# Gate rows spread over the partitions by a stride-zero DRAM read, with each head's exponent and mask taken into the head before

## The chip, the cores and the metric

One core of a Trainium2 chip runs the kernel. The metric is the device time of one execution in microseconds (us). The engines are named as in the profile: PE (TensorE, matmuls; PEld its weight loads), ACT (ScalarE), DVE (VectorE), POOL (GpSimd), SP (SyncE, which here only issues DMA transfers). Transfers are also issued by ACT.

## The reference

One encoder layer over 2048 prompt tokens and 64 sample tokens, model width 1024. Four pooling channel groups and four mLSTM heads of width 128 share one input projection and one output projection; a gated feed-forward part with a causal convolution follows. The change concerns the mLSTM:

```
b    = cumsum(log_sigmoid(f gate));  dmat[t,s] = b[t] - b[s] + ig[s]   (s <= t)
inter = b + m;  m_t = max(inter, max_s dmat)
wt   = exp(dmat - m_t)
a    = wt * (q . k)
num  = a @ v + exp(inter - m_t) * (C q);   den likewise with n
h    = num / max(|den|, exp(-m_t))
C, n are carried from chunk to chunk
```

Then each head is normalized and multiplied by the sigmoid of the o projection. The kernel splits dmat - m_t into a part per row (b - m_t at t, called r) and a part per column (ig - b at s): wt[s,t] = exp(r[t] + c[s]), with chunks of 128 tokens.

## The kernel before, in words

The attention phase takes the first 735 us of the span. It handles the tokens in four groups of 512 (the last with the 64 sample tokens besides, 576 columns). The feed-forward phase fills the rest and isn't touched.

All large products are made as three fp32r matmuls of high and low halves (`gemm`, line 460). A weight block arrives as `raw` by a DMA on SP, ACT copies it to its high half (line 394) and DVE subtracts to get the low half (line 397); `work_out` does this some blocks ahead.

For each group, `proj_v` makes v for all heads (`va`) and the gate columns. Then the generator `gate_rows` turns the gates into rows of 4 heads x 512 tokens, in small steps: r, the running maximum M, and the columns `CL` (c, and three exponentials) and `GL` (the chunk's carry factor on all partitions). For each head, `proj_qko` makes q, k and th (tanh of o), evacuated from PSUM by ACT (line 1246), and the generator `lstm` does the head's own work. Both generators stand in a queue bg[0]; `gemm` calls `tick(0)` at five places of a weight row, and each tick runs one step, up to the next `yield`. So a head's lstm lies between the matmuls of the next head's projections, and gate_rows between those of the first head's. Other queues hold the pooling, the next group's norm, and, on DVE, the sums of conditioning weights (`ada`, line 210). `fold` (lines 887, 888: 8 small products with WPT, folded into w_out) runs beside group 0 only, in steps taken by `extra()`.

In lstm, r has to stand on all 128 partitions. It does so by a matmul (line 1292): the one-hot column `E_r[:, hd]`, taken with stride zero as a 128-column weight, times `RHL`, where rows 0 to 3 hold the high half of r and rows 32 to 35 its low half. ACT takes Exp of the product from PSUM for each of four chunks, with the column c as its bias, into `at`; DVE takes the minimum with a causal mask. Then come, in order: transposes of k (line 1305) and `kw` on DVE, q.k (line 1315) and at times it; the products kw with va that advance the state (line 1330, `st`); the products of state and at with q and va (lines 1350, 1352), from which ACT and DVE make `nd`; a square `jk` on ACT for each chunk; the scale `sf` (DVE, and a power on POOL); nd times sf. The closing transposes of nd (line 1384) are done by `end()`, which is kept in `ends` and called in the next head.

PSUM: four large banks for projections (mm_ps), and four single ones for everything else (m2_ps, `m` in the profile), which are handed out in turn: the k-th request waits until the (k-4)-th has been read. Instructions wrapped in `Urgent` are shown at line 233. Group 0 is placed by a scheduler on its estimates; the work of groups 1 to 3 follows mostly the order of the code.

Of the kernel before, what the change touches and what calls it, by code (L numbers as in the profile page):

```python
# [9 lines left out]
F32 = mybir.dt.float32  # L10
F32R = mybir.dt.float32r
AF = mybir.ActivationFunctionType
# [53 lines left out]
def tile_layer(ctx: ExitStack, tc: tile.TileContext, xT, vecs, cst, rst, w_mod, w_ada, c_rows, w_qkou, w_v, w_pool,  # L66
# [21 lines left out]
    def m2_ps():  # L88
        return bank("m2")
# [11 lines left out]
    def scr():  # L101
        return sp.tile([P, TMAX], F32, tag="scr", name="scr")
# [717 lines left out]
    if True:  # L820
# [270 lines left out]
        E_r = a1.tile([P, NH], F32R, tag="E_r", name="E_r")  # L1091
        R4 = a1.tile([P, TMAX], F32, tag="R4", name="R4")
        pool.memset(R4, 0.0)
        RHL = a1.tile([P, TMAX], F32R, tag="RHL", name="RHL")
        pool.memset(RHL.bitcast(F32), 0.0)
# [65 lines left out]
        def gate_rows(o, gt, cols):  # L1161
# [53 lines left out]
            act.activation(RHL[0:4, :T], r[:4, :T], AF.Copy)  # L1215
            dve.tensor_tensor(out=RHL[32:36, :T], in0=r[:4, :T], in1=RHL[0:4, :T].bitcast(F32), op=ALU.subtract)
            for _ in range(8):
                yield
# [21 lines left out]
            cols += [CL, GL]  # L1240
# [32 lines left out]

        ends = []

        def lstm(o, hd, qko, va, cols, mix):
# [3 lines left out]
            CL, GL = cols  # L1280
            at = a2.tile([P, WIDE], F32, tag="at", name="at")
            if o.last:
                pool.memset(at[TS:, GT:TMAX], 0.0)
                pool.memset(at[:, TMAX:], 0.0)
# [4 lines left out]
            for (a, b, n, s) in o.tsegs:  # L1289
                lo, w = a * P, (b - a) * n  # L1290
                pr = m2_ps()
                pe.matmul(pr[:n, :w], E_r[:, hd:hd + 1].broadcast_to([P, n]), RHL[:, lo:lo + w], start=True, stop=True)
                for ti in range(a, b):
                    c0 = (ti - a) * n
                    act.activation(at[:n, ti * P:ti * P + n], pr[:n, c0:c0 + n], AF.Exp, bias=CL[:n, ti, 0, hd:hd + 1])

                av = at[:n, lo:lo + w].rearrange("p (t c) -> p t c", c=n)
                dve.tensor_tensor(out=av, in0=av, in1=mask[:n, :n].unsqueeze(1).broadcast_to([n, b - a, n]), op=ALU.min)
            if o.last:
                yield  # L1300
# [20 lines left out]
            extra()  # L1321
            yield
# [42 lines left out]
            for (a, b, n, s) in o.tsegs:  # L1365

                den = nd[:n, a:b, 128]
                dve.tensor_tensor(out=sf[:n, a:b], in0=den, in1=den, op=ALU.mult)
                dve.tensor_tensor(out=sf[:n, a:b], in0=sf[:n, a:b], in1=CL[:n, a:b, 2, hd], op=ALU.max)
                dve.scalar_tensor_tensor(out=sf[:n, a:b], in0=sf[:n, a:b], scalar=EPS, in1=sq[:n, a:b],  # L1370
                                         op0=ALU.mult, op1=ALU.add)
                pool.tensor_tensor(out=sf[:n, a:b], in0=sf[:n, a:b], in1=half[:n, :b - a], op=ALU.pow)
# [81 lines left out]
        for o in groups:  # L1454
# [16 lines left out]
            if o.g == 0:  # L1471
                t = scr()
                nc.sync.dma_start(out=t[:P, :NH], in_=cst[:P, NCST + 512:NCST + 512 + NH])
                dve.tensor_copy(E_r, t[:P, :NH])
# [757 lines left out]
def _constants():  # L2232
    c = np.zeros((P, NCST + 512 + NH), np.float32)
# [8 lines left out]
    for h in range(NH):  # L2242
        c[h, NCST + 512 + h] = c[32 + h, NCST + 512 + h] = 1.0
# [72 lines left out]
```

## Time and profile before

| what | value |
|---|---|
| time, median of 3 runs | 2164.13 us (2162.03 to 2164.81) |
| the profiled execution: its time, its span | 2170.81 us, 2169.0 us |
| granted TensorE clock, mean | 0.998 |
| PE busy | 2143.5 us, 99% of the span |
| DVE, ACT, POOL busy | 1629.1 us (75%), 1096.2 us (51%), 250.5 us (12%) |
| the broadcast matmuls (line 1292) | 20, 0.40 us long each for 512 columns |
| the Exps of `at` | 68 instructions, 19.0 us |
| DMA in the attention phase | 215.83 MB, 294 GB/s |

The profiled execution is the one that the rows come from; its own time stands 6.7 us over the median of the runs. A row of the timeline begins with its start in us from the span's start and its duration; in brackets stand the idle time of the engine before it and what ended it. In a list of waits the numbers are us in total, how many times, and the longest. A row of line 233 is told apart by its tiles: `at<-m,CL` is the Exp, `at<-at,mask` the mask, `kw<-m,CL` the weighting of k.

### The profile page before, as it was taken

Reading aid. Unit: us, or ns where it says so; the run is one execution under the profiler, and the core shown is the slowest. Engines: PE = TensorE matmul, PEld = TensorE weight load, DVE = VectorE, ACT = ScalarE, POOL = GpSimd, SP = SyncE. Lnnn points to the kernel's source line nnn. Section 1 sums busy time; section 2 is a strip of 40 time slices with the busy share of each in tenths; the row PEclk is TensorE's granted clock in tenths of the full one; section 3 lists DMA queues with packets and bytes.
Section 4 is the critical chain, followed back from the end, with each engine's and each line's share of the span. In section 5 each row is a group of like instructions: output and inputs, shape, how many; then the busy total and the mean of one; then the engine's idle time right before and its main releaser. Section 6 shows DMA issues by size and latency. Waiting matters only on the chain.

```text
span 2169.0 us, 37946 instructions
## 1 busy us (share of the span) xinstructions
PE 2143.5 (99%) x13488; PEld 2042.9 (94%) x13488; DVE 1629.1 (75%) x3068; ACT 1096.2 (51%) x2182; POOL 250.5 (12%) x499
## 2 busy tenths in 40 slices
PE   8999999999999999999999999999999999999998
PEld 7788988888899999999999999999999999999998
DVE  5678768767964868797957668988876597887874
ACT  4555235334333546464736455655655365565554
POOL 0000000002000101010101120100100331111112
PEclk9999999999999999999999999999999999999999
DMA  8897998988886576889977976666678675555542
GB/s 306 305 327 256 336 338 279 354 319 292 279 306 221 168 261 219 303 279 313 331 225 244 322 265 196 229 224 199 221 232 264 217 260 183 174 174 189 174 160 79
DMA packets 245862, 543.63 MB, mean 251 GB/s; under 512 B 25252, under 2 KB 68772, under 8 KB 242856
## 3 DMA queue, kind: packets, MB, share of 16 engines
q1 hardware_dynamic: 236232, 518.89, 70.6%
q10 hardware_dynamic: 9440, 22.32, 2.6%
q8 instruction: 106, 1.74, 0.3%
q14 instruction: 84, 0.69, 0.1%
HBM read 415.12 MB, written 125.99 MB: 249 GB/s over the span
## 4 chain that ended last, share of the span: by engine, by line
PE 71%; DVE 8%; DMA 4%; issue 2%; ACT 2%; SPq 0%; POOL 0%; DVEq 0%; POOLq 0%; ACTq 0%
PE mm L1595 33%; PE mm L460 14%; PE mm L2161 12%; PE mm L2038 8%; DVE wt L397 2%; DMA wt<-wsum 1%; PE mm L1129 1%; DMA raw<-w_ada 1%; DVE tg L1573 1%; ACT tg L1568 0%; PE m L1350 0%; PE m L1330 0%; PE m L1352 0%; DVE scr L233 0%; DMA wsum<-w 0%
## 5 line engine op out<-in xcount | busy, mean ns | idle before, releaser
L1595 PE MATMUL mm<-hx,wt 128*128 128x352 f32 x5544 | 888.6, 321 | 1.6 <-DVE eg L1604 1.6
L1595 PEld LDWEIGHTS mm<-hx,wt 128*128 128x128 f32 x5544 | 881.9, 188 | 2.9 <-ACT wt L394 1.3
L460 PE MATMUL mm<-hl,wt 128*128 128x512 f32 (+2 forms) x1920 | 388.4, 357 | 0.8 <-ACT va L233 0.8
L394 ACT ACTIVATE wt<-raw 128x512 fp32r<-128x512 f32 (+3 forms) x470 | 276.8, 597 | 169.6 <-PE mm L2161 47.7
L460 PEld LDWEIGHTS mm<-hl,wt 128*128 128x128 f32 x1920 | 315.7, 189 | 43.9 <-ACT va L233 1.0
L397 DVE TENSOR_TENSOR wt<-raw,wt 128x512 fp32r<-128x512 f32 (+3 forms) x470 | 312.7, 671 | 47.8 <-ACT wt L394 47.0
L2161 PE MATMUL mm<-av,wt 128*128 128x448 f32 (+1 forms) x1632 | 262.7, 322 | 0.0
L2161 PEld LDWEIGHTS mm<-av,wt 128*128 128x128 f32 x1632 | 250.4, 188 | 11.1
L2010 DVE SCALAR_TENSOR_TENSOR x<-mm,MOD,x 128x352 f32<-128x352 f32 (+3 forms) x360 | 167.4, 504 | 78.6 <-PE mm L2161 65.1
L2038 PE MATMUL mm<-av,wt 128*128 128x352 f32 x1344 | 220.8, 323 | 2.5 <-DVE ea L1604 0.9
L2038 PEld LDWEIGHTS mm<-av,wt 128*128 128x128 f32 x1344 | 215.4, 188 | 5.6 <-DVE ea L1604 3.6
L1642 ACT ACTIVATE mm<-mm 128x352 f32<-128x352 f32 x196 | 87.8, 448 | 250.3 <-PE mm L1595 194.0
L460 PE MATMUL mm<-mx,wt 128*128 128x512 f32 (+1 forms) x960 | 183.1, 352 | 0.4 <-DVE scr L233 0.3
L460 PEld LDWEIGHTS mm<-mx,wt 128*128 128x128 f32 x960 | 159.4, 189 | 23.3 <-issue 0.5
L1573 DVE SCALAR_TENSOR_TENSOR ta<-ea,V,ta 128x704 f32<-128x704 f32 (+1 forms) x132 | 125.7, 952 | 64.4 <-ACT ta L1568 51.6
L1573 DVE SCALAR_TENSOR_TENSOR tg<-eg,V,tg 128x704 f32<-128x704 f32 (+1 forms) x132 | 125.7, 952 | 62.0 <-ACT tg L1568 59.7
L397 DVE TENSOR_TENSOR wt<-wt 128x512 fp32r<-128x512 f32 x196 | 132.8, 684 | 12.9 <-ACT wt L394 12.9
L394 ACT ACTIVATE wt<-wt 128x512 fp32r<-128x512 f32 x196 | 119.8, 623 | 36.2 <-DMA wt<-wsum 32.0
L1551 POOL COPY ea<-UC 128x2 f32<-128x2 f32 x66 | 32.9, 499 | 484.8 <-DVE ta L1573 397.0
L1782 ACT ACTIVATE tg<-tg 128x704 f32<-128x704 f32 (+1 forms) x66 | 52.5, 795 | 71.2 <-DVE tg L1573 71.2
L1129 PE MATMUL mm<-wt,hl 128*128 128x256 f32 (+1 forms) x576 | 71.1, 284 | 0.0
L1129 PEld LDWEIGHTS mm<-wt,hl 128*128 128x128 f32 x576 | 70.3, 190 | 0.6 <-issue 0.4
(298 smaller groups left out, 2173.5 us busy)
## 6 DMA issues: line engine op xcount, KB each, us to landing
wt<-wsplit SPq DMA_DIRECT2D x132, 512.0 KB, 4.5
raw<-w_up SPq DMA_DIRECT2D x198, 256.0 KB, 4.0
wt<-hl_kept SPq DMA_DIRECT2D x96, 512.0 KB, 5.9
wt<-wsum SPq DMA_DIRECT2D x132, 256.0 KB, 4.9
wsplit<-wt SPq DMA_DIRECT2D x66, 512.0 KB, 5.5
w<-w_up SPq DMA_DIRECT2D x44, 512.0 KB, 5.1
wsum<-w SPq DMA_DIRECT2D x22, 1024.0 KB, 4.8
Bd<-fscr ACTq DMA_DIRECT2D x56, 352.0 KB, 4.3
```

Source lines behind the costliest of these rows:

```text
L394: act.activation(u.w[:, 0, :u.n], u.raw[:, :u.n], AF.Copy)
L397: dve.tensor_tensor(out=u.w[:, 1, :u.n], in0=u.raw[:, :u.n], in1=u.w[:, 0, :u.n].bitcast(F32), op=ALU.subtract)
L460: pe.matmul(ps[bi][:, :hi - lo], U[:, a, k % 4 * P:(k % 4 + 1) * P], mv[k][:, b, lo:hi], start=(at == 0 and pi == 0), stop=(k == order[-1] ...
L1129: pe.matmul(ps[ti][:n, :cols], h[4 * kh + k4][:, b, lo:lo + n], U[:, a, k4 % 2 * cols:(k4 % 2 + 1) * cols], start=(kh == 0 and k4 == 0 and ...
L1551: pool.tensor_copy(ext[:, 0:2], UC[:, f, :])
L1573: dve.scalar_tensor_tensor(out=t[:, :E], in0=ext[:, j:j + E], scalar=wc(j, f), in1=t[:, :E], op0=ALU.mult, op1=ALU.add)
L1595: pe.matmul(bk.t[:, :FH], U[:, a, kc * P:(kc + 1) * P], Bo.at(nm, kc, b), start=(first and kc == 0 and pi == 0), stop=(kc == 3 and pi == 2 ...
L1642: act.activation(to.t[:, :FH], bk.t[:, :FH], AF.Copy)
L1782: act.activation(self.tg[:, :E], self.tg[:, :E], AF.Silu)
L2010: dve.scalar_tensor_tensor(out=x3[n][:, a:b], in0=bk.t[:, a - lo:b - lo], scalar=gt2(n, s), in1=x3[n][:, a:b], op0=ALU.mult, op1=ALU.add)
L2038: pe.matmul(bk.t[:, :FH], U[:, a, c:c + P], quad.put(op, m, b), start=(first and m == 0 and pi == 0), stop=(m == 1 and pi == 2), skip_grou ...
L2161: pe.matmul(bks[i].t[:, :hi - lo], U[:, a, k % 4 * P:(k % 4 + 1) * P], av[k][:, b, lo:hi], start=(k == 0 and (a, b) == PASSES[0]), stop=(k ...
```

## The change

`gate_rows` writes r to a DRAM buffer `rd` by a DMA that ACT issues, where it wrote RHL. `at_tile` loads one head's row of rd into an SBUF tile on all 128 partitions: the source is taken with stride zero, 256 KB arrive (and 64 x 64 more in the last group). `decay` takes the Exp in place, SBUF to SBUF, and the mask. For head 0 the load is issued four steps after the write and decay stands at the end of gate_rows; for head hd+1 the load is issued in head hd's lstm after `extra()`, and decay stands at the end of head hd's lstm. RHL, E_r, their preparation, the 20 matmuls and one `yield` of the last group are gone, and with them one request of a small bank for each head (two in the last group).

```diff
-            act.activation(RHL[0:4, :T], r[:4, :T], AF.Copy)
-            dve.tensor_tensor(out=RHL[32:36, :T], in0=r[:4, :T], in1=RHL[0:4, :T].bitcast(F32), op=ALU.subtract)
-            for _ in range(8):
+            rd = dr.tile([4, TMAX], F32, tag=f"rd{o.g}", name=f"rd{o.g}")
+            act.dma_start(out=rd[:, :T], in_=r[:4, :T])
+            for _ in range(4):
+                yield
+            spread = [at_tile(o, rd, 0)]
+            for _ in range(4):
                 yield
...
-            cols += [CL, GL]
+            cols += [CL, GL, rd, spread]
+            decay(o, spread[0], CL, 0)
...
+        def at_tile(o, rd, hd):
+
+            load = Urgent(nc.scalar).dma_start
+            t = a2.tile([P, WIDE], F32, tag="at", name="at")
+            if o.last:
+                load(out=t[:, :GT], in_=rd[hd:hd + 1, :GT].broadcast_to([P, GT]))
+                load(out=t[:TS, GT:TMAX], in_=rd[hd:hd + 1, GT:TMAX].broadcast_to([TS, TS]))
+                pool.memset(t[TS:, GT:TMAX], 0.0)
+                pool.memset(t[:, TMAX:], 0.0)
+            else:
+                load(out=t[:, :o.T], in_=rd[hd:hd + 1, :o.T].broadcast_to([P, o.T]))
+            return t
+
+        def decay(o, at, CL, hd):
+
+            for (a, b, n, s) in o.tsegs:
+                lo, w = a * P, (b - a) * n
+                for ti in range(a, b):
+                    cell = at[:n, ti * P:ti * P + n]
+                    tc.keep_in_program_order(nc.scalar.activation(cell, cell, AF.Exp, bias=CL[:n, ti, 0, hd:hd + 1]))
+                av = at[:n, lo:lo + w].rearrange("p (t c) -> p t c", c=n)
+                tc.keep_in_program_order(nc.vector.tensor_tensor(
+                    out=av, in0=av, in1=mask[:n, :n].unsqueeze(1).broadcast_to([n, b - a, n]), op=ALU.min))
...
-            for (a, b, n, s) in o.tsegs:
-                lo, w = a * P, (b - a) * n
-                pr = m2_ps()
-                pe.matmul(pr[:n, :w], E_r[:, hd:hd + 1].broadcast_to([P, n]), RHL[:, lo:lo + w], start=True, stop=True)
-                for ti in range(a, b):
-                    c0 = (ti - a) * n
-                    act.activation(at[:n, ti * P:ti * P + n], pr[:n, c0:c0 + n], AF.Exp, bias=CL[:n, ti, 0, hd:hd + 1])
-
-                av = at[:n, lo:lo + w].rearrange("p (t c) -> p t c", c=n)
-                dve.tensor_tensor(out=av, in0=av, in1=mask[:n, :n].unsqueeze(1).broadcast_to([n, b - a, n]), op=ALU.min)
-            if o.last:
-                yield
...
             extra()
+            if hd < NH - 1:
+                spread.append(at_tile(o, rd, hd + 1))
             yield
...
+            if spread:
+                decay(o, spread[0], CL, hd + 1)
```

In the order of the instructions, the first place is ACT in group 0, from the row r being ready to the first head's Exp (`rd` is the DRAM buffer, `scr_725` and `scr_731` hold r, `raw` and `wt` are weight blocks). Before:

```order
L233 ACTIVATE RHL_183<-scr_731 4x512
L394 ACTIVATE wt_863<-raw_796 128x512
L394 ACTIVATE wt_901<-raw_821 128x512
L1246 ACT_TABLE_LOAD
L1246 ACTIVATE th_843<-mm_844 128x512
L233 ACTIVATE CL_883<-m2_885 128x4x4 x3
L394 ACTIVATE wt_919<-raw_848 128x512
L394 ACTIVATE wt_967<-raw_866 128x512
L1246 ACTIVATE q_899<-mm_900 128x512
L233 ACTIVATE at_979<-m2_982,CL_883 128x128 x4
```

And now:

```order
L233 DMA rd0_807<-scr_725 4x512
L394 ACTIVATE wt_859<-raw_790 128x512
L233 DMA at_851<-rd0_807 128x512
L394 ACTIVATE wt_897<-raw_815 128x512
L233 DMA at_995<-rd0_807 128x512
L1247 ACT_TABLE_LOAD
L1247 ACTIVATE th_837<-mm_838 128x512
L233 ACTIVATE CL_879<-m2_881 128x4x4 x3
L394 ACTIVATE wt_915<-raw_842 128x512
L1294 ACTIVATE at_851<-at_851,CL_879 128x128 x4
L394 ACTIVATE wt_968<-raw_862 128x512
L1247 ACTIVATE q_895<-mm_896 128x512
```

The write of r stands where the copy into RHL stood, the loads for heads 0 and 1 stand between the weight copies behind it, and the Exps of head 0 stand ahead of one weight copy and the q evacuation that they followed before.

The second place is PE in group 0, from the fold's first two blocks to head 0's closing transposes (`q_713` and `q_707` are head 0's q, `q_899` and `q_895` head 1's; `nd_981` is head 0's result). Before:

```order
L887 MATMUL m2_1018<-w4_767,WPT_177 128x128 x4
L1350 MATMUL m2_1053<-st2_1013,q_713 128x129
L1352 MATMUL m2_1053<-va_689,at_979 128x129
L460 MATMUL mm_1145<-hl6_577,wt_1117 128x512 x2
L887 MATMUL m2_1072<-w4_767,WPT_177 128x128 x4
L1315 MATMUL m2_1174<-q_899,k_965 128x128 x4
L1330 MATMUL m2_1194<-va_689,kw_1159 128x129
L1384 MATMUL mm_1181<-V_96,nd_981 128x128 x4
```

And now:

```order
L887 MATMUL m2_1013<-w4_761,WPT_177 128x128 x4
L1362 MATMUL m2_1040<-SP0_184,q_707 128x129
L1364 MATMUL m2_1040<-va_686,at_851 128x129
L1362 MATMUL m2_1040<-st0_1004,q_707 128x129
L460 MATMUL mm_1145<-hl7_575,wt_1117 128x512
L887 MATMUL m2_1067<-w4_761,WPT_177 128x128 x4
L460 MATMUL mm_1145<-hl7_575,wt_1117 128x512 x2
L1315 MATMUL m2_1160<-V_96,k_966 128x128 x4
L1342 MATMUL m2_1188<-va_686,kw_1158 128x129 x3
L1342 MATMUL m2_1198<-va_686,kw_1158 128x129
L1399 MATMUL mm_1173<-V_96,nd_981 128x128 x4
```

Behind the first fold block stood head 0's last two products, and now stand its first three, with head 1's transposes of k, its four kw products and head 0's closing transposes behind the second block.

The third place is ACT at the same point in the program (`sq` gathers a chunk's sum of squares; line 888 evacuates the fold, line 908 squares the next group's x). Before:

```order
L888 ACTIVATE w4_767<-m2_1018 128x512
L233 ACTIVATE nd_981<-m2_1053 128x129
L233 ACTIVATE jk_1070,sq_1044<-nd_981 128x128
L888 ACTIVATE w4_767<-m2_1072 128x512
L394 ACTIVATE wt_1216<-raw_1096 128x512
```

And now:

```order
L888 ACTIVATE w4_761<-m2_1013 128x512
L233 DMA at_1183<-rd0_807 128x512
L233 ACTIVATE nd_981<-m2_1040 128x129
L888 ACTIVATE w4_761<-m2_1067 128x512
L233 ACTIVATE jk_1053,sq_1039<-nd_981 128x128
L394 ACTIVATE wt_1210<-raw_1091 128x512
L233 ACTIVATE jk_1057,sq_1039<-nd_981 128x128
L908 ACTIVATE ssum_1077<-mx0_948 128x512
L233 ACTIVATE jk_1061,sq_1039<-nd_981 128x128
L908 ACTIVATE mx0_948<-mx0_948 128x512
L233 ACTIVATE jk_1065,sq_1039<-nd_981 128x128
```

One of head 0's four squares stood here, and now all four stand here, between other instructions and behind the load for head 2.

More of the change, by code (lines that the diff above doesn't have):

```diff
@@ L1090, in tile_layer @@
         mask = a1.tile([P, P], F32, tag="mask", name="mask")
-        E_r = a1.tile([P, NH], F32R, tag="E_r", name="E_r")
         R4 = a1.tile([P, TMAX], F32, tag="R4", name="R4")
         pool.memset(R4, 0.0)
-        RHL = a1.tile([P, TMAX], F32R, tag="RHL", name="RHL")
-        pool.memset(RHL.bitcast(F32), 0.0)
         M = a1.tile([4, TMAX + 2], F32, tag="M", name="M")
@@ L1279, in lstm @@
             q, k, th = qko
-            CL, GL = cols
-            at = a2.tile([P, WIDE], F32, tag="at", name="at")
-            if o.last:
-                pool.memset(at[TS:, GT:TMAX], 0.0)
-                pool.memset(at[:, TMAX:], 0.0)
+            CL, GL, rd, spread = cols
+            at = spread.pop()
             kw = a2.tile([P, 5, P], F32, tag="kw", name="kw", bufs=1)
@@ L1288, in lstm @@
             nd = a2.tile([P, 5, 129], F32, tag="nd", name="nd")
-            for (a, b, n, s) in o.tsegs:
-                lo, w = a * P, (b - a) * n
-                pr = m2_ps()
-                pe.matmul(pr[:n, :w], E_r[:, hd:hd + 1].broadcast_to([P, n]), RHL[:, lo:lo + w], start=True, stop=True)
-                for ti in range(a, b):
-                    c0 = (ti - a) * n
-                    act.activation(at[:n, ti * P:ti * P + n], pr[:n, c0:c0 + n], AF.Exp, bias=CL[:n, ti, 0, hd:hd + 1])
-                av = at[:n, lo:lo + w].rearrange("p (t c) -> p t c", c=n)
-                dve.tensor_tensor(out=av, in0=av, in1=mask[:n, :n].unsqueeze(1).broadcast_to([n, b - a, n]), op=ALU.min)
-            if o.last:
-                yield
             for (a, b, n, s) in o.tsegs:
@@ L1470, in tile_layer @@
                 va = proj_v(o, h, cols)
[L1471 to L1474, printed above, removed]
             if o.g == 0:
@@ L2232, in _constants @@
 def _constants():
-    c = np.zeros((P, NCST + 512 + NH), np.float32)
+    c = np.zeros((P, NCST + 512), np.float32)
     c[127, C_L127:C_L127 + P] = 1.0
@@ L2241, in _constants @@
     c[:, NCST:NCST + 512] = np.tile(m, (1, 4))
-    for h in range(NH):
-        c[h, NCST + 512 + h] = c[32 + h, NCST + 512 + h] = 1.0
     return c
```

## The prediction

> **What bounds the kernel now.** I read the page's busy line and its chain of work first, then the waits of the matrix engine in the attention phase, where all of the change lies.
>
> ```profile
> PE 2143.5 (99%) x13488; PEld 2042.9 (94%) x13488; DVE 1629.1 (75%) x3068; ACT 1096.2 (51%) x2182; POOL 250.5 (12%) x499
> ...
> PE 71%; DVE 8%; DMA 4%; issue 2%; ACT 2%; SPq 0%; POOL 0%; DVEq 0%; POOLq 0%; ACTq 0%
> ```
>
> PE works for 99% of the span, and 71% of the chain that ended last is PE. So a matmul that goes is worth what PE spends on it, and everything else in the change (Exp, mask, transfers) counts only where PE is made to wait. The waits of PE in the first 800 us:
>
> ```profile
> PE m L1330 <- DVE kw L233: 3.8, 3, 2.7
> PE mm L1384 <- DVE nd L233: 1.9, 2, 1.1
> ```
>
> Nowhere in that list does PE wait for the Exp or the mask that the change moves. Its waits are for kw (the weighted k) and for nd (a head's normalized result), both written by DVE. The two waits that the change can touch most stand in token group 0, whose order a scheduler makes.
>
> **What is removed from PE.** The one-hot matmul of line 1292, and what it costs in place: from its start to the next matmul's start.
>
> ```profile
> L1292 PE MATMUL m<-RHL,E_r x20: 196/395/397, 73.8 to 701.5; 128*128 128x512 f32 x16, 128*64 128x64 f32 x4
> ...
> 260.24 0.40 PE L1292 MATMUL m<-RHL,E_r 128*128 128x512 f32 x1
> 260.48 0.60 PE L1305 MATMUL m<-V,k 128*128 128x128 f32 x4
> ...
> 624.22 0.43 PE L1292 MATMUL m<-RHL,E_r 128*128 128x512 f32 x2
> 624.49 1.03 PE L460 MATMUL mm<-hl,wt 128*128 128x256 f32 x6
> ```
>
> Each reads 0.40 us long but holds PE for 0.24 (260.24 to 260.48); a big and a small one together hold it for 0.27 (624.22 to 624.49). 16 x 0.24 + 4 x 0.03 = 4.0 us, 0.18% of the time. That is all the change can take from PE directly.
>
> **What comes off ACT and DVE.** The copy of r into RHL and the subtraction behind it go from both engines, and the Exp now reads SBUF in place of PSUM. I cost these at nothing: in groups 1 to 3 they lie beside PE's projections, as these rows of group 1 show.
>
> ```profile
> 244.46 0.63 ACT L233 ACTIVATE RHL<-scr 4x512 fp32r<-4x512 f32 x1 [0.67 <-DVE scr L233]
> ...
> 259.07 0.60 ACT L1246 ACTIVATE th<-mm 128x512 f32<-128x512 f32 x1 [1.90 <-PE mm L460]
> ...
> 260.68 1.14 ACT L233 ACTIVATE at<-m,CL 128x128 f32<-128x128 f32 x4 [1.01 <-PE m L1292]
> ```
>
> ACT has r at 244.46, and the four Exps stand at 260.68: 16 us, in which ACT waits for PE more than it works. If that cover went, the price would be the 1.14 of the Exps, once a group.
>
> **What comes in: transfers.** One of 8 KB out of SBUF and, for each head, one of 256 KB with the stride-zero source, all issued by ACT. The trace has no write followed by such a read, but it has its neighbours:
>
> ```profile
> L815 ACTq DMA_DIRECT2D Bd<-fscr x56: 326/326/350, 879.7 to 1629.5; - x56
> ...
> u<-cs SPq DMA_DIRECT2D x2, 256.0 KB, 6.3
> cs<-gap SPq DMA_DIRECT2D x1, 8.0 KB, 3.9
> ```
>
> An issue takes ACT 0.33 us, the 8 KB write of conditioning rows landed after 3.9 us, and loads of the same 256 KB broadcast shape landed after 6.3 (between 40 and 200 us, the busy part). So the way from r to the spread row is 0.33 + 3.9 + 0.33 + 6.3 = 10.9 us. In groups 1 to 3 there are 16 us, so it is hidden with 5 to spare; later heads load a whole head ahead. In group 0 the write issues where RHL's copy stood:
>
> ```profile
> 64.12 0.63 ACT L233 ACTIVATE RHL<-scr 4x512 fp32r<-4x512 f32 x1 [0.61 <-DVE scr L233]
> ...
> 75.64 0.63 ACT L394 ACTIVATE wt<-raw 128x512 fp32r<-128x512 f32 x1 [4.24 <-DMA raw<-w_qkou]
> ...
> 76.30 0.69 DVE L397 TENSOR_TENSOR wt<-raw,wt 128x512 fp32r<-128x512 f32 x1 [0.82 <-ACT wt L394]
> ...
> 78.25 0.09 DVE L210 DVE_READ_ACCUMULATOR2_ANT MOD<- 128x1 f32 x1
> 78.25 0.69 DVE L233 TENSOR_TENSOR kw<-m,CL 128x512 f32<-128x512 f32 x1
> ...
> 79.00 2.09 PE L1330 MATMUL m<-va,kw 128*128 128x129 f32 x8 [2.75 <-DVE kw L233]
> ```
>
> 64.12 + 10.9 = 75.0, and the Exp now stands ahead of the weight copy that starts at 75.64: in time by half a microsecond. This chain (weights land, ACT copies, DVE subtracts, two passes of the conditioning sum, kw, PE) stays whole, so kw comes when it came, PE arrives 0.24 earlier, and that 0.24 is given back. The 0.52 MB of new traffic can push the landing at 75.64: from 0 to 1.4 us (0.52 MB at the 384 GB/s that the DMA moved here, row below). I take the middle, +0.7.
>
> By the Trainium skill ("DMA: Bandwidth & Descriptors", section "Anatomy of one DMA"), a transfer costs about 2.0 us and its bytes at 436 GB/s, and a semaphore wait sits on the sequencer that issues. By that estimate the two trips take 4.6 us in place of 10.2, and the +0.7 would shrink rather than grow; the rows above are longer, being taken under load, and I stay with them. The second half of the rule speaks against the change: ACT itself stands until the write has landed; that is the second rival.
>
> **What is moved: group 0, from head 0 to head 1.** With one PSUM tile less for each head, the rotation of the four small banks shifts, and head 0's first three products now come behind the fold matmuls (line 887). Behind them PE finds transposes, four kw products and then head 0's closing transposes, which need nd, with only three projection matmuls in between. The same chain before:
>
> ```profile
> 97.15 1.05 PE L887 MATMUL m<-w,WPT 128*128 128x128 f32 x8
> 98.04 0.39 PE L1350 MATMUL m<-st,q 128*128 128x129 f32 x2
> 98.24 0.60 ACT L888 ACTIVATE w<-m 128x512 f32<-128x512 f32 x1 [1.92 <-PE m L887]
> 98.27 0.39 PE L1352 MATMUL m<-va,at 128*128 128x129 f32 x2
> ...
> 98.74 0.27 ACT L233 ACTIVATE nd<-m 128x129 f32<-128x129 f32 x1
> ...
> 99.43 0.31 ACT L233 ACTIVATE jk<-nd 128x128 f32<-128x128 f32 x1 [0.42 <-DVE nd L233]
> ...
> 99.90 0.17 DVE L233 SCALAR_TENSOR_TENSOR sf<-sf,sq 128x4 f32<-128x4 f32 x1
> ...
> 101.10 0.62 ACT L908 ACTIVATE ssum<-mx 128x512 f32<-128x512 f32 x1
> ...
> 101.19 0.69 DVE L233 TENSOR_TENSOR nd<-nd,sf 128x512 f32<-128x512 f32 x1 [1.13 <-POOL sf L1372]
> 101.62 0.62 ACT L908 ACTIVATE mx<-mx 128x512 f32<-128x512 f32 x1
> ...
> 101.94 0.66 PE L1384 MATMUL mm<-V,nd 128*128 128x128 f32 x4 [0.72 <-DVE nd L233]
> ```
>
> Now with the new order, counted from the first fold matmul. PE: 0.89 for the fold (97.15 to 98.04), 3 x 0.23 for head 0's products (98.04 to 98.27), a second fold 0.89, three projection matmuls 0.7 (0.24 each, as for the broadcast of the same width), transposes 0.43 (as the distance 260.48 to 260.91), four kw products 0.92: 4.5 us of work. The chain that nd takes: fold evacuation until 1.7, the new load's issue 0.33, nd's copy at 2.0, second fold evacuation (it ends at 3.5), then on ACT four squares (0.31 and the reading of the sum, some 0.4 each) between a weight copy and two norm squares (0.52 each, 101.10 to 101.62): the last square starts at 6.3; from there 0.47 to sf, 1.29 to nd, 0.75 to PE: 8.8. So PE loses 4.3 us here, in two pieces: about 1.0 for kw, 3.3 for nd. Before, all squares but the last were done long ahead, and it lost 0.72 (I count 0.8). Net +3.5, between +2.5 and +5.
>
> **What a wait costs beyond its length.** The wait at 76.25 to 79.00 is followed by this (us, PE busy, granted clock, DMA share, GB/s by microsecond):
>
> ```profile
> 77.00:78.00 1.00, 0.00 (x0) 1.00 1.06 399
> ...
> 79.00:80.00 1.00, 1.00 (x4) 0.50 1.06 430
> ...
> 81.00:82.00 1.00, 1.00 (x4) 0.50 1.04 373
> ...
> 83.00:84.00 1.00, 1.00 (x6) 1.00 1.00 369
> ```
>
> After 2.75 us of idleness PE was granted half its clock for about 3.4 us (0.91, 0.50, 0.50, 0.50, 0.88 over five microseconds), which loses 1.7. The new wait of 3.3 us is longer, so I add +1.7; the other end is 0, since one case doesn't show how idle a stretch must be. This row is the nearest, and the idleness it shows is shorter than the one I expect, so I take its value.
>
> The Trainium skill ("TensorE: Matmul & The Clock Gate", Part 1) has a free-running window of 3413 ns, and the clock halves after at least one idle window. Taken by the letter, 3.3 us can't fill a window, and the sum would be 1.7 lower, 2162.6; the rows at 79 agree on the length of the slow stretch and on the half, but show that 2.75 us of idleness is enough.
>
> **Small waits.** Three others are touched:
>
> ```profile
> 123.28 0.91 PE L1330 MATMUL m<-va,kw 128*128 128x129 f32 x6 [0.52 <-DVE kw L233]
> ...
> 162.06 0.66 PE L1384 MATMUL mm<-V,nd 128*128 128x128 f32 x4 [1.15 <-DVE nd L233]
> ...
> 284.26 0.94 PE L1330 MATMUL m<-va,kw 128*128 128x129 f32 x6 [0.51 <-DVE kw L233]
> ```
>
> At 284.26 the kw now stands one conditioning pass earlier on DVE, and the wait goes (-0.5); at 123.28 I take -0.3. At 162.06 nine more projection matmuls (9 x 0.24) stand ahead of the closing transposes, and the 1.15 goes.
>
> **The sum:** -4.0 + 0.24 + 0.7 + 3.5 + 1.7 - 0.8 - 1.15 = +0.2 us. The feed-forward phase (735 us to the end) keeps its order, 0. The profiled execution lasted 2170.81, 6.7 above the median of 2164.13; the sum was made from its rows and is put on the median: 2164.3.
>
> **The rivals.**
> A: the wait between head 0 and 1 is covered, because the squares are issued tighter or PE reaches nd later. For it: before, the same place cost only 0.72. Against: the instructions' order on PE and ACT leaves 4.5 us of work against a chain of 8.8. Then 3.5 and 1.7 go: 2159.1, faster by 0.23%; it decides once the chain is under 5.3 us.
> B: slower. ACT stands in its own queue until the write has landed and then for the spread row; both trips lie just within their cover. If each takes 2 us longer than in the rows, the spread row is there at 79.0 in place of 75.0, Exp and mask end at 80.8, and kw, behind the mask on DVE, reaches PE 3.5 later; with the weight copy behind the first issue late too, up to 5. That gives 2168 to 2169.3. It starts to count from 11.5 us for both trips. For it: the DMA was busy at 1.0 of its share here. Against: the measured 3.9 and 6.3 are from the same stretch.
> C: the clock keeps up in the new wait: 2162.6, no change by measurement.
>
> **How the numbers follow.** A measurement of this kernel tells 0.2%, 4.3 us, from no change: faster is below 2159.8, slower above 2168.5. I give my sum 0.34 and C, whose time reads as no change too, 0.22; A, with whatever else makes it faster, 0.18; B 0.16; and 0.10 for both waits longer than worked out (5 and a second clock drop: 2168 to 2171). Range 2157.5 to 2170.5: at the low end A with the +0.7 gone and the small waits better, at the high end B's 5 on top of the sum and a little more.
>
> **What the profile afterwards would show.** Line 1292's group is gone and PE has 20 matmul records less in the attention phase. PE waits for nd at about 103 us for some 3 us, and the clock by microsecond reads 0.50 behind it. PE still waits at 76 for 2.75 to 3.5 us, for kw. The waits at 162 and 284 are gone; groups 1 to 3 show no wait for the spread rows. I am wrong if the write and the load show longer landings than 3.9 and 6.3 in group 0, if nd is there when PE comes, or if the feed-forward phase changes its length.

## The result, and the profile after

The changed kernel takes 2172.28 us (median of 6 runs, 2169.34 to 2175.68), the kernel before in the same comparison 2164.47 us (6 runs, 2162.03 to 2169.60). The ratio is 1.0029, 95% interval 1.0019 to 1.0040: slower by 0.29%, some 6 us (the two medians differ by 7.8). The forecast was 2164.3 with a range up to 2170.5, so the time lies outside it, on the slow side.

The profiled execution of the changed kernel took 2171.95 us (span 2170.2 us), close to its median. First the page's busy line and its chain of work:

```profile
PE 2138.6 (99%) x13468; PEld 2039.6 (94%) x13468; DVE 1627.0 (75%) x3063; ACT 1091.5 (50%) x2178; POOL 244.3 (11%) x498
...
PE 77%; DVE 9%; DMA 8%; issue 2%; ACT 2%; SPq 1%; POOL 0%; DVEq 0%; ACTq 0%; POOLq 0%
```

PE has its 20 matmuls less, as the change says, and the kernel is slower all the same. The 4.9 us less of busy time are not the gain: a second profile of before (below) reads 2138.2. The profile that the prediction used, with 2143.5, had a stretch of halved clock (1.7 us lost) and a slow stretch in the feed-forward phase (last section), and both count as busy. The gain stays the 4.0 us that the 20 matmuls held PE for. In the chain, DMA has gone from 4% to 8%. So the loss must be in waits, and the list of PE's waits in the attention phase (60 to 800 us, with total, count and longest) has them:

```profile
PE m L1342 <- DVE kw L233: 6.8, 4, 4.5
PE mm L1399 <- DVE nd L233: 2.7, 1, 2.7
PE m L1364 <- DVE SN L233: 1.6, 1, 1.6
PE m L887 <- DMA w<-w_out: 0.9, 1, 0.9
PE mm L460 <- DMA wt<-hl_kept: 0.8, 1, 0.8
...
```

The one of 4.5 us for kw is head 0's in group 0, the one of 2.7 for nd stands between heads 0 and 1 of that group. Line 1342 here is line 1330 of before, 1399 is 1384. SN (the state behind the sample tokens, in the last group), w_out (the load of a block of w_out for the fold) and hl_kept (kept halves of weights that are loaded again) are new in this list.

The kernel before was profiled a second time in the last comparison (2163.54 us, span 2161.8, where the median was 2164.22 of 12 runs). Its list over the same stretch (one comment line was added at the top of the file, so every line number is one higher):

```profile
PE m L1331 <- DVE kw L234: 2.2, 2, 1.8
PE mm L1385 <- DVE nd L234: 1.8, 2, 1.1
PE mm L461 <- ACT va L234: 1.5, 1, 1.5
...
```

This matters for all that follows. In the profile that the prediction was made from, the same kw wait was 2.75 us with a halved clock behind it; here it is 1.76 and the clock stays at full speed:

```profile
76.00:77.00 1.00, 0.00 (x0) 1.00 1.00 399
77.00:78.00 1.00, 0.84 (x7) 1.00 1.01 402
```

(Each row: stretch, its length, PE busy with the number of matmuls, granted clock, DMA share, GB/s.) The first profile was of an execution 6.7 us above the median, the second is of one near it. In the changed kernel the clock is halved behind both long waits:

```profile
80.00:81.00 1.00, 0.44 (x2) 0.50 0.99 369
81.00:82.00 1.00, 1.00 (x7) 0.50 1.03 395
82.00:83.00 1.00, 1.00 (x5) 0.50 1.04 397
83.00:84.00 1.00, 1.00 (x5) 0.81 1.05 404
...
107.00:108.00 1.00, 0.51 (x3) 0.64 0.99 399
108.00:109.00 1.00, 1.00 (x6) 0.50 1.10 440
109.00:110.00 1.00, 1.00 (x4) 0.50 0.61 250
110.00:111.00 1.00, 1.00 (x4) 0.66 0.00 0
```

Summing one minus the granted clock over 60 to 180 us gives 3.4 us lost after the change, 1.7 in the first profile of before, 0 in the second. Of the 3.4, 0.4 fall in time in which PE still waits (80.00 to 80.56, 107.27 to 107.49), so 3.0 are lost by matmuls.

To see where the time stands, I compared the start of the n-th projection matmul (line 460) and of the n-th feed-forward matmul in two profiles. Start of the changed kernel's minus before's, in us:

| place | against the first profile | against the second |
|---|---|---|
| 49 us (first projection) | +0.6 | +0.9 |
| end of group 0 (about 240 us) | +4.3 | +7.9 |
| end of group 1 (415 us) | +3.9 | +7.8 |
| end of attention (732 us) | +4.2 | +7.4 |
| end of the kernel (span) | +1.2 | +8.4 |

Against the second profile the account closes. Group 0 (60 to 243 us): PE's waits 9.1 against 4.0 (+5.1), clock +3.0, four matmuls gone at 0.24 (-1.0), together +7.1; measured 7.0 (7.9 less the 0.9 at its start). Groups 1 to 3: waits 4.6 against 2.0 (+2.6), sixteen matmuls gone, four of them small (-3.0), together -0.4; measured -0.5. The feed-forward phase adds 1 us, which lies within what it varies from one profile to another (last section). So the 4 us taken from PE were lost twice: in groups 1 to 3 to small new waits, and in group 0 to two long ones and the slow clock behind them.

Why kw of head 0 is late shows in the timelines of SP, ACT and DVE of the changed kernel:

```profile
63.22 0.52 ACTq L233 DMA_DIRECT2D rd<-scr  x1
...
65.59 0.37 ACTq L233 DMA_DIRECT2D at<-rd  x1
...
66.03 0.51 ACTq L233 DMA_DIRECT2D at<-rd  x1
...
63.88 3.95 SPq L193 DMA_DIRECT2D w<-w_ada  x2
67.93 0.38 SPq L373 DMA_DIRECT2D raw<-w_qkou  x1
...
74.44 0.63 ACT L394 ACTIVATE wt<-raw 128x512 fp32r<-128x512 f32 x1 [4.43 <-DMA raw<-w_qkou]
74.97 1.27 ACT L1294 ACTIVATE at<-at,CL 128x128 f32<-128x128 f32 x4
...
75.10 0.69 DVE L397 TENSOR_TENSOR wt<-raw,wt 128x512 fp32r<-128x512 f32 x1 [3.32 <-ACT wt L394]
...
78.45 0.68 DVE L1296 TENSOR_TENSOR at<-at,mask 128x512 f32<-128x512 f32 x1
...
79.72 0.69 DVE L233 TENSOR_TENSOR kw<-m,CL 128x512 f32<-128x512 f32 x1
```

and of before, second profile:

```profile
63.17 0.33 SPq L194 DMA_DIRECT2D w<-w_ada  x1
63.59 0.38 SPq L374 DMA_DIRECT2D raw<-w_qkou  x1
...
67.50 0.33 SPq L194 DMA_DIRECT2D w<-w_ada  x1
...
69.30 0.38 SPq L374 DMA_DIRECT2D raw<-w_qkou  x1
...
71.00 0.69 DVE L398 TENSOR_TENSOR wt<-raw,wt 128x512 fp32r<-128x512 f32 x1
...
74.47 0.69 DVE L398 TENSOR_TENSOR wt<-raw,wt 128x512 fp32r<-128x512 f32 x1 [0.55 <-ACT wt L395]
...
76.42 0.69 DVE L234 TENSOR_TENSOR kw<-m,CL 128x512 f32<-128x512 f32 x1
```

The scheduler moved more than the lines of the diff. SP now issues a second conditioning load (`w_ada`) ahead of a raw weight block. That load can't go out until DVE has done with its buffer, and SP stands there (63.88 to 67.83 for the two loads): the block is issued at 67.93 where it was at 63.59. At the same time the two spread rows of 256 KB are on their way (ACT issues them at 65.59 and 66.03), and the block lands after 6.48 us, at 74.41. DVE stands 3.32 us in front of that block's line 397 (75.10). Before, it had the same block without a wait (71.00) and stood only 0.55 in front of the next one (74.47). What queues behind (conditioning passes, a second line 397, the mask, kw) slides along: kw starts at 79.72 in place of 76.42.

### The profile page after: what moved, and what is told of

Its sections match the earlier page's. It is cut to its first block, busy times and chain, and to the rows that moved or that the text cites. A ratio compares the mean times of both kernels' runs of the same rounds, so it can differ in the third digit from the quotient of the medians.

```text
span 2170.2 us, 37947 instructions
## 1 busy us (share of the span) xinstructions
PE 2138.6 (99%) x13468; PEld 2039.6 (94%) x13468; DVE 1627.0 (75%) x3063; ACT 1091.5 (50%) x2178; POOL 244.3 (11%) x498
## 4 chain that ended last, share of the span: by engine, by line
PE 77%; DVE 9%; DMA 8%; issue 2%; ACT 2%; SPq 1%; POOL 0%; DVEq 0%; ACTq 0%; POOLq 0%
PE mm L1606 34%; PE mm L460 17%; PE mm L2172 12%; PE mm L2049 8%; DVE wt L397 2%; DMA raw<-w_ada 2%; DMA wt<-wsum 1%; DVE scr L233 1%; DMA wsum<-w 1%; DVE junk L210 1%; DMA at<-rd 1%; PE m L1342 1%; PE m L1364 1%; PE m L1362 1%; DVE tg L1584 1%
```

## Experiments

Twelve kernels ran, in three comparisons; before's medians there were 2164.85, 2166.33 and 2165.75 us. Theory Q: the cost is in group 0, in the order that the scheduler gives to the queues (the rotation of the small banks, and the loads on SP). Rivals: it is the transfers themselves, or the Exp and mask put at another place.

**1 and 2. Group 0 as before, or only group 0 changed.** Both paths stand in the file and are chosen by the group:

```diff
+        def by_matmul(o):
+            return o.g == 0        # second kernel: o.g > 0
...
+            if by_matmul(o):       # the lines of before
...
-            if hd < NH - 1:
+            if hd < NH - 1 and not by_matmul(o):
```

> Group 0 is as before (matmul spreading, Exp and mask in place), groups 1 to 3 are as changed. Theory 1 (the loss lies at two places of group 0, and in groups 1 to 3 new small waits just eat the 2.9 us of PE that are saved): the time is that of before within 1.5 us, attention phase -1 to +1 us, PE still waits for kw, k, kept weights and SN in groups 1 to 3, 3 to 4 us in all. Theory 2 (the added transfers slow the phase wherever they run): 2 to 4 us slower than before, as three of four groups still have them.

> Group 0 is as changed, groups 1 to 3 are as before. Theory 1: nearly the whole loss is here: 4 to 6 us slower than before, PE waits 4.5 us for kw at 76 us and 2.7 for nd at 105 us. Theory 2: 1 to 2 us slower, a quarter of the loss.

With group 0 as before: 2166.47 us, ratio 1.0011 (1.0002 to 1.0019). With only group 0 changed: 2170.92, 1.0038 (1.0024 to 1.0051), as slow as the whole change; kw waits 3.68 and nd 2.71 there, and 5.1 us are lost to the halved clock. So most of the loss is in group 0. But the other three groups, with 16 of the 20 matmuls gone, gained nothing; they read 0.11% slower. PE's waits in the attention phase of the first kernel:

```profile
PE m L1375 <- DVE kw L233: 3.3, 3, 2.0
PE mm L460 <- DMA wt<-hl_kept: 2.1, 2, 1.3
PE mm L1432 <- DVE nd L233: 1.8, 2, 1.1
PE m L1397 <- DVE SN L233: 1.2, 1, 1.2
...
```

The waits for hl_kept and SN are the ones that the changed kernel has too, and the lists of before have neither.

**3. The bank rotation of before.** One request for a small bank, unused, for each head and segment, so that the four banks are handed out as they were:

```diff
             nd = a2.tile([P, 5, 129], F32, tag="nd", name="nd")
+            for _ in o.tsegs:
+                m2_ps()
```

> The changed kernel, with one small bank for each head requested and not used, so that the rotation of the small banks is that of before. Theory 1: the products of head 0 come ahead of the fold again, the wait for nd at 105 us falls from 2.7 to under 1 us and the clock stays up there: 4 to 5 us faster than the changed kernel, so 1 to 3 slower than before; the 4.5 us wait for kw at 76 us stays. Theory 2: no different from the changed kernel, 6 us slower than before.

2168.23 us, 1.0014 (1.0005 to 1.0023). The nd wait between the heads falls from 2.71 to 0.49 and no halved clock follows it; kw still waits, and the clock stays halved for two stretches behind that one wait (3.4 us lost):

```profile
79.86 2.09 PE L1344 MATMUL m<-va,kw 128*128 128x129 f32 x8 [4.24 <-DVE kw L233]
...
104.33 0.66 PE L1401 MATMUL mm<-V,nd 128*128 128x128 f32 x4 [0.49 <-DVE nd L233]
```

So the shifted rotation is what puts nd in PE's way, and the kw wait has another cause.

**4. The transfers added to before.** r is written and head 0's row read back with stride zero into a DRAM buffer that nobody uses, while the matmuls stay:

```diff
+            rd = dr.tile([4, TMAX], F32, tag=f"rd{o.g}", name=f"rd{o.g}")
+            act.dma_start(out=rd[:, :T], in_=r[:4, :T])
...
-            for _ in range(8):
+            for _ in range(4):
+                yield
+            spare_load(o, rd, 0)     # rd, stride zero, into DRAM
+            for _ in range(4):
                 yield
```

> The kernel before, with the write of r and one spreading read for each group (into DRAM, 256 KB, unused) issued by ACT where the changed kernel issues them for its first head; all computation as before. Theory 1: ACT stands until the write has landed (1.5 us in group 0, 4 in the others), a weight block comes late in group 0 and PE's wait for kw at 76 us grows from 2.75 by 1 to 2 us, groups 1 to 3 lose under 1: 1 to 3 us slower than before. Rival (kw comes late because the mask now stands ahead of it on DVE): kw waits 2.75 as before, no change in time.

2170.31 us, 1.0024 (1.0012 to 1.0036): slower, and yet kw waits only 1.31 and the clock isn't halved. Against the second profile of before it is 2.4 us late at the end of attention and 4.6 more in the feed-forward phase, where this edit does nothing and whose length varies by 5.0 from profile to profile (last section). The trace names two waits there (1.1 for ACT to read a product, 0.8 for a weight) and not why. This stays open. Since these reads write DRAM, which the change's don't, it can't be taken as the change's price; nor does it rule out that the change's own transfers cost something.

**5. The order on SP alone.** Before, with the raw weight loads of the early blocks kept in the program's order, so that SP issues the second conditioning load ahead of the block as in the changed kernel:

```diff
-            nc.sync.dma_start(out=u.raw[:, :u.n], in_=src)
+            keep_in = tc.keep_in_program_order if pos[0] < 20 else (lambda i: i)
+            keep_in(nc.sync.dma_start(out=u.raw[:, :u.n], in_=src))
```

> The kernel before, with one thing changed: on SP the second of two conditioning loads (line 193) goes ahead of a weight load of group 0, the order that the changed kernel has there. Theory P (kw of head 0 comes late because SP, which issues in order, holds a weight load behind a conditioning load whose buffer is not yet free; the block lands 3 to 4 us later and DVE's queue with kw stands behind it): PE's wait for kw at 76 us grows to 3.5 to 4.5 us (1.3 to 2.75 so far in kernels with the other order), 2 to 4 us slower than before. Rival M (kw is late because the mask stands ahead of it on DVE): the mask stands behind kw here, so the wait stays at 1.3 to 2.75 and the time is that of before.

2165.81 us, 1.0000 (0.9991 to 1.0009), kw waits 1.53: the swap without the new transfers costs nothing that can be measured. I had taken it for the cause; alone it isn't.

**6. Rotation and loads.** The changed kernel with experiment 3's lines, and the conditioning loads issued one at a time, a step later:

```diff
-                if i % 2 == 0 and i < len(todo):
-                    w = quarter()
-                    for d in range(2):
-                        got[i + d] = w[:, d]
-                        tc.keep_in_program_order(nc.sync.dma_start(out=w[:, d], in_=w_ada[m - 2, i + d]))
+                if i < len(todo):
+                    if i % 2 == 0:
+                        w = quarter()
+                        got[i], got[i + 1] = w[:, 0], w[:, 1]
+                    tc.keep_in_program_order(nc.sync.dma_start(out=got[i], in_=w_ada[m - 2, i]))
...
-        lead = 4 if quarter else 3
+        lead = 3
```

> The changed kernel with the rotation of the small banks as before and with the conditioning loads of group 0 issued one by one and one step later, so that both weight loads stand ahead of the pair on SP. Theory P: PE's wait for kw at 76 us falls from 4.2 (same_rotation) to 2 us or less, though the mask still stands ahead of kw; group 0 ends level with before or 1 to 2 us earlier, the time is 2 to 4 us better than same_rotation, so before's within 1.5 us. Rival M: the wait stays near 4, no gain over same_rotation.

2165.66 us, 0.9999 (0.9991 to 1.0008); kw waits 1.05 with the mask still ahead of kw on DVE, so the mask's place alone doesn't make kw late. The clock stays full in group 0; it is halved once in the last group (633 to 637 us), behind a wait of 1.88 for SN.

**7. The loads alone.** The same edit of the conditioning loads, with the rotation left as the change has it.

> The changed kernel, with only the conditioning loads (w_ada) issued one at a time and a step later, as in rotation_and_loads, and the bank rotation left as the change has it. SP then issues the raw weight load ahead of the second w_ada load again. Theory R+L (two causes of about equal size, the late weight in front of head 0's kw, and the shifted rotation between head 0 and head 1): kw of head 0 waits 1 to 2 us in place of 4.5, no halved clock at 80 us, the nd wait between the heads stays at 2 to 3 us or moves with the new order; time 2167 to 2170. Rival L alone (the late weight explains it all, and the rotation's gain in same_rotation was chance): 2165 to 2166.5, level with before. Rival R alone: no better than 2171.

2167.29 us, 1.0007 (0.9997 to 1.0017). The block is issued at 64.09 again:

```profile
64.09 0.33 SPq L373 DMA_DIRECT2D raw<-w_qkou  x1
...
67.53 1.55 SPq L193 DMA_DIRECT2D w<-w_ada  x2
...
77.87 1.13 PE L1342 MATMUL m<-va,kw 128*128 128x129 f32 x8 [2.01 <-DVE kw L233]
...
101.97 0.66 PE L1399 MATMUL mm<-V,nd 128*128 128x128 f32 x4 [2.48 <-DVE nd L233]
```

The kw wait is 2.01, the nd wait stays, and neither is followed by a halved clock here. The four corners, as ratios to before: the change 1.0029, with the rotation of before 1.0014, with the loads 1.0007, with both 0.9999. Each part takes away about half, in the traces as in the times. The intervals of neighbouring corners overlap, and the last step, 1.0007 to 0.9999, is shown by the nd row rather than by the time.

**8. The second spread row held back.** The changed kernel with the loads of heads 1 to 3 kept in the program's place in groups 0 to 2:

```diff
+            elif hd:
+                tc.keep_in_program_order(load(out=t[:, :o.T], in_=rd[hd:hd + 1, :o.T].broadcast_to([P, o.T])))
             else:
                 load(out=t[:, :o.T], in_=rd[hd:hd + 1, :o.T].broadcast_to([P, o.T]))
```

> The changed kernel, with the spread-row loads of heads 1 to 3 kept in the program's place in groups 0 to 2, so that in group 0 head 1's 256 KB load isn't issued beside head 0's at 65 us. If the second 256 KB load delays the raw weight (traffic): raw lands 1 to 2 us earlier, the kw wait of head 0 falls from 4.5 to 2.5 to 3.5, and the time to 2169 to 2171. If the weight is late only because SP issues it behind the second w_ada load: the wait stays at 4 to 4.5 and the time at 2171 to 2173. If these loads cost through groups 1 to 3 (the hl_kept wait at 440 us): that wait goes, 0.8 less.

For the disputed wait the answer is clear. SP issues the block at the late place still (67.38), but with one spread row under way in place of two it lands after 3.84 us, not 6.48, and kw's wait falls to 2.50:

```profile
63.34 3.95 SPq L193 DMA_DIRECT2D w<-w_ada  x2
67.38 0.42 SPq L373 DMA_DIRECT2D raw<-w_qkou  x1
...
71.24 0.63 ACT L394 ACTIVATE wt<-raw 128x512 fp32r<-128x512 f32 x1 [1.79 <-DMA raw<-w_qkou]
...
77.65 1.76 PE L1344 MATMUL m<-va,kw 128*128 128x129 f32 x8 [2.50 <-DVE kw L233]
```

Set side by side, the kw waits speak for both being needed together: late issue with two spread rows 4.47 (the changed kernel), 4.24 (experiment 3) and 3.68 (only group 0 changed), late issue with one row 2.50, late issue with none 1.53 (experiment 5), early issue with two rows 2.01 and 1.05 (experiments 7 and 6). Each is from one profiled execution, and over the seven profiles of kernels whose group 0 spreads r by the matmul this wait is 1.12 to 2.75, so only the waits of 3.68 and more stand clear of it. The hl_kept wait at 440 us is gone too, so it comes with these loads. The time went the other way, to 2177.14 us, 1.0048 (1.0032 to 1.0063): holding the loads gave group 0 yet another order, with new waits for the fold (line 887: 1.9 for w_out, 2.2 for ACT) and for nd (1.55 and 1.64), and a second halved clock at 153 us, behind the 1.9. I had expected 2169 to 2173.

**9 and 10. Repairs.** Group 0 as before (kernel 1), or experiment 6's edits, each with the loads of heads 1 to 3 kept in place in groups 1 and 2 and the last group's `yield` put back.

> As g0_matmul, but in groups 1 and 2 the load for head 1 is kept behind head 0's Exps (it went out together with head 0's, 512 KB at once), and the last group keeps the step that the change removed. Theory L (the two loads at once push back the kept weight blocks in group 2, and without the step the SN of the last group stands on DVE behind a wait for a weight sum's load): the waits for kept weights (2.1 us in g0_matmul) and SN (1.2 us) fall under 0.5 each, 2 to 3 us faster than g0_matmul, 1 us faster than before or level. Rival (these waits come with any such load): they stay, time as g0_matmul, 1 to 2.5 us slower than before.

> rotation_and_loads together with the late loads and the kept step of g0_matmul_late_loads. If the places named are all there is, PE's saved 4.0 us come out: 2 to 4 us faster than before (2161 to 2163). If transfers cost something of themselves, it stays level with before or slower.

2166.14 us, 1.0004 (0.9994 to 1.0014), and 2165.32, 1.0000 (0.9990 to 1.0009). In both the hl_kept wait shrinks or goes, and others come (st 1.5 and kw 3.8 in total in the second). All repairs together bring the change level with before; none brings a gain, though PE does 4 us less of work. From 60 to 735 us PE stands idle for 8.1 us with all repairs and for 6.0 in the second profile of before, which accounts for 2 of the 4; whether the transfers cost the rest stays open.

**11 and 12. Controls.** Before with only the write of r added, which nobody reads; and before unaltered.

> The kernel before, with only the 8 KB write of r to DRAM on ACT's queue in each group; nobody reads it. write_and_load_added was 0.24% slower and its profile did not show where. If ACT is held by the write until it lands: ACT has a gap of 2 us or more behind the issue in each group and the time is that of write_and_load_added, 2169 to 2171. If the 256 KB reads (their traffic, or the shift they give to the order of later loads) were the cost: level with before, 2164.5 to 2166.5.

> The kernel before, unaltered, as a measure of what no change reads as: ratio 1.0000 within 0.001. In its profile the kw wait of head 0 is 2.5 to 3 us with a halved clock at 79 to 82 us, if that is usual; the feed-forward phase is 1376 to 1381 us long, with its stretches of 166.7 ns matmuls at other places than in the first profile, if those come by execution.

The write alone: 2164.27 us, 0.9991 (0.9979 to 1.0002). No change: 2164.22, 0.9996 (0.9986 to 1.0006). So the write costs nothing that can be measured, and kernels level with before read within 0.1%. The kw wait of the unaltered kernel, expected at 2.5 to 3 us, was 1.76.

## Why the prediction was wrong, and where it was right

**The base.** One step that failed: "the sum was made from its rows and is put on the median". Against the profile that it was made from, the sum looks nearly right, +0.2 forecast and +1.2 between the two spans, but that is luck: at the end of attention, where all its terms lie, the changed kernel is 4.2 us late, and the feed-forward phase, which the change doesn't touch, was 3.0 shorter. The 4 us by which the attention phase misses are mostly the waits of groups 1 to 3 (2.7 more than in that profile, where 0.5 less was forecast), then kw (0.8 more than forecast) and a first projection that starts 0.6 later. And that execution stood 6.7 us over the median, and the prediction moved the sum down by all of that without asking what the 6.7 were. The second profile tells: 3.6 of them stand at the end of group 0 (mostly the longer kw wait and the 1.7 of halved clock), and most of the rest in a slow stretch of the feed-forward phase (last section). The changed kernel has a long kw wait and the halved clock in its usual execution, so it didn't come down with the median: its mean granted clock is 0.996 or 0.997 in all six runs, where 96 runs of before show 0.998 or 0.999 in 84 and 0.997 in 12.

**"This chain stays whole, so kw comes when it came", +0.24 and +0.7 for traffic.** Wrong, and the largest single cost: the wait was 4.47, where 2.75 + 0.94 = 3.69 was forecast. Against the 1.76 of the second profile it is 2.7 longer, and with the clock behind it 2.7 + 1.7 = 4.4 us in place of 0.9; part of that is the base. The prediction looked at ACT's and DVE's place in this chain and bounded the transfer by bytes. Its chain starts at the block that ACT copies at 75.64, and the block that came late is the one ahead of it, which cost DVE no wait before. It didn't look at SP, which issues that block: the order of SP had changed there, and SP stood in its queue until 67.83. Of the 3.3 us by which kw is later, 2.8 are DVE's longer stand for weight blocks (3.32 against 0.55), and 0.6 the mask ahead of kw.

**Between heads 0 and 1: +3.5, and +1.7 for the clock.** Right in mechanism and close in size: 1.0 and 3.3 forecast for kw and nd, 0.78 and 2.71 measured, with the clock halved behind it at 107 to 111. Experiment 3 shows the cause named there, the rotation of the banks.

**Groups 1 to 3, "hidden with 5 to spare".** The trips themselves were hidden: the spread row landed in a median of 4.3 us where 6.3 was taken, and PE never waits for the Exp or mask there. What was missed is what else they disturb: hl_kept 0.76, SN 1.57, kw 1.01 and 0.49. The price per matmul (0.24) was right, and of the gain from it, 3 us, most was given back to these. In the repaired kernels hl_kept shrinks or goes where the loads are kept in place; what lies behind the others was not tested one by one. The prediction had the wait at 284 gone; it is there at 288.65 with 1.01. The wait at 162 went as forecast, and one for w_out at 151 (0.94) came.

**The rivals.** A (no wait between the heads) and C (the clock keeps up) did not happen. B gave the right side, though its 2168 to 2169.3 falls short of 2172.28, and the right victim, kw behind a late chain, by the wrong road (its 3.5 for kw is 2.6 by the rows that it names, 80.8 against 78.25). ACT did stand in its queue for the write, but for 1.54 us, since r landed 2.4 us after its issue. Nearest came the last case, with both waits longer than worked out, 2168 to 2171 at 0.10. ACT's rows:

```profile
66.00 0.63 ACT L394 ACTIVATE wt<-raw 128x512 fp32r<-128x512 f32 x1 [1.54 <-DMA rd<-scr]
...
424.29 0.27 ACTq L233 DMA_DIRECT2D rd<-scr  x1
...
428.61 0.83 ACTq L233 DMA_DIRECT2D at<-rd  x2
429.49 0.60 ACT L1247 ACTIVATE q<-mm 128x512 f32<-128x512 f32 x1 [4.50 <-DMA rd<-scr]
```

In group 2 the same write took 4.3 us (424.29 to 428.61) and held ACT for 4.50. The Trainium skill ("DMA: Bandwidth & Descriptors", section "Anatomy of one DMA — SWDGE (gpsimd) path") has a fixed cost of about 2.0 us for a transfer, fitted on transfers that GpSimd issues, where ACT issues these; an estimate from it for 8 KB is 2.0 us. The 2.4 is near that, the 4.3 is twice as long. The Exps started at 74.97, behind the weight copy and not behind the spread row: it was in time, and a queue one step further back was not.

## What to carry to other kernels

Where a scheduler places the work, compare the order on every queue, the transfer queues too, and follow each block that the bound engine needs back to the place where it is issued; here the new loads cost more by what stood behind them than by their bytes. Work taken from an engine that is 99% busy is a gain only if its suppliers have slack at that place: here DVE and SP had none, and 4 us less of matmuls gave no gain that can be measured even when repaired. Before a sum is put on the median, ask which rows of the profile are of that one execution. And when a sum agrees with the difference of two spans, see whether it also agrees where its terms lie.

## What the runs showed of the hardware

**When the clock halves.** Waits of PE of 1.9 and 2.50 (experiment 8), 1.88 (experiment 6), 2.04 (experiment 1), 2.71 and 2.75 us were followed by half the clock for about 3.4 us (1.7 us lost). Waits of 1.76 (second profile of before), 2.01 and 2.48 (experiment 7), and 2.2 (experiment 8) were not. Rows of experiment 7 behind its wait of 2.48:

```profile
101.00:102.00 1.00, 0.03 (x1) 1.00 1.02 375
102.00:103.00 1.00, 1.00 (x8) 1.00 1.00 320
```

So between 1.9 and 2.5 us it can fall either way, and the traces show what decides: where the wait lies on a grid. In every trace the steps of the granted clock stand whole multiples of 3.413 us apart. In the changed kernel the first record of the clock, at full speed, starts at 11.70 us, and the clock changes at 79.97, 83.38, 107.27 and 110.69, which is 20, 21, 28 and 29 such stretches later. Counted in these stretches, the wait of 2.48 leaves 1.76 us of idleness in one and 0.72 in the next, that of 2.01 leaves 1.50 and 0.51, that of 2.2 leaves 0.99 and 1.20; the 2.04 of experiment 1 lies in one stretch whole. Over all fourteen traces, but for their last 20 us, it comes out like this for stretches at full clock: behind one with 1.85 us or more of idleness the next always ran at half, behind one with less than 1.5 it never did, and of nine with 1.50 to 1.76 one was followed by half the clock (1.54, experiment 9).

Waits of 3.68 and 4.24 cost two such stretches, 3.4 us; the one of 4.47 in the changed kernel cost one. Here too the place counts: in the stretch already halved, the first two leave 0.98 and 0.72 us of idleness, the last 0.59. The Trainium skill ("TensorE: Matmul & The Clock Gate", Part 1) has a free-running window of 3413 ns, and the traces agree with that; its "≥1 idle window" is more than was needed, since 1.85 us of idleness in a window of 3.41 were enough here.

**Two paces of the same matmuls.** In the feed-forward phase, matmuls of 352 columns follow each other about every 158 ns, and in some stretches of some executions every 166, with PE busy throughout and the clock granted in full. The same 50 us (1605 to 1655) in the first profile of before, then in the second, then in the changed kernel:

```profile
1605.00:1655.00 50.00, 50.00 (x302) 1.00 0.75 250
```

```profile
1605.00:1655.00 50.00, 50.00 (x317) 1.00 0.79 263
```

```profile
1605.00:1655.00 50.00, 49.98 (x316) 1.00 0.76 252
```

50 us / 302 = 166 ns against 50 / 317 = 158. Such stretches go with a feed-forward phase of 1375.6 to 1380.6 us (from the last projection matmul to the end of the last matmul) over the fourteen profiles, and the first profile of before had one of the longer ones. PE's waits in that phase are 5.5 to 7.2 us, so they make up at most 1.7 of the 5. What sets the pace isn't known.
